# A PSUM bank for each direction in the block merges of a triangular inverse

## The chip, the cores and the metric

The kernel runs on one core of one Trainium2 chip. The metric is the device time of one execution in microseconds (us); of several runs the median counts.

## What is computed

One layer of a bidirectional hybrid encoder on x (1024 tokens, 1024 channels, float32): an input projection feeds eight heads of neighbourhood attention and four heads of gated DeltaNet in two directions; both are mapped by an output projection, and a mixture of 64 experts (two per token) follows. The change lies in the DeltaNet part. Per direction, head and chunk of 64 tokens the reference solves a unit lower triangular system and carries a state over the chunks:

```python
lower = jnp.where(strict, jnp.einsum('bhnid,bhnjd->bhnij', kb, k) * decay, 0.0)
a_mat = jnp.eye(c, dtype=f32) + lower
sol = lax.linalg.triangular_solve(a_mat, rhs, left_side=True, lower=True, unit_diagonal=True)
u, w = sol[..., :dv], sol[..., dv:]
def step(state, inp):
    v_new = u_c - jnp.einsum('bhck,bhkv->bhcv', w_c, state)
    o_c = (jnp.einsum('bhck,bhkv->bhcv', q_c * jnp.exp(g_c)[..., None], state)
           + jnp.einsum('bhij,bhjv->bhiv', qk_c, v_new))
    state = (state * jnp.exp(g_last)[..., None] + ...)
```

## The kernel before

The kernel is one long function, recorded in source order and then put in order by a scheduler: on each engine instructions may stand far from their source neighbours, and once that order is fixed each engine works through it strictly, so that an instruction which waits holds up all behind it. Which PSUM tiles share a bank, and what depends on what, enters into the scheduler's order. So an edit of a few lines can move instructions of other stages.

The kernel inverts the 64x64 triangular matrices itself. VectorE (DVE) inverts the two 32x32 diagonal blocks of 64 matrices (16 chunks by 4 heads) for each of the two directions by substitution (L457, L460). Then come the **merges**: the off-diagonal 32x32 block is minus the product of three 32x32 blocks. The 64 matrices go in four groups g of 16. Stage one of a group is 32 small matmuls, 16 of direction 0 (L483, operands in partitions 0 to 31, result in PSUM partitions 32 to 63) and 16 of direction 1 (L484, operands in 96 to 127, result in 64 to 95), in alternation. ScalarE (ACT, L485) and DVE (L486) copy the results to `wt`. Stage two is the same with L489 and L490, and ACT (L491) and DVE (L492) write the block to `TT`. A DMA on GpSimd's queue (POOL, L493) stores the group to `T_d` in DRAM. A stage's results of both directions share one PSUM bank `pw` or `px`, taken in turn from the pool `psB` of five.

The matmuls of the **natural projections** (L84, L85, L86 in `mm3`) fill TensorE (PE) meanwhile; their weights are loaded by SP (L74, `w_raw`) and split by ACT (L75) and DVE (L76). Their q and k blocks are normalised: ACT squares (L402), DVE reduces (L403, L404), POOL takes the power -0.5 (L51, the function `rsqrt`), DVE scales (L406), PE transposes (L417), and ACT and DVE take the result out of PSUM (L421, L422).

After the merges comes the **scan** over 16 chunks, a chain: PE multiplies the state (`pk`, L529), DVE makes `r` (L531, eight instructions), PE multiplies by the inverse (`pw`, L536), ACT and DVE copy the result (`wc`, L537 and L538), PE makes the state's update (`ps`, L545), DVE the new state (`sn`, L551). Outputs (L559, L556, L563) and the natural projections lie between. Attention, the output projection, the router and the experts come after.

Of the kernel before, what the change touches and what calls it, by code (L numbers as in the profile page):

```python
# [8 lines left out]
F32 = mybir.dt.float32  # L9
# [3 lines left out]
AF = mybir.ActivationFunctionType  # L13
OP = mybir.AluOpType
# [5 lines left out]
P = 128  # L20
# [16 lines left out]
def tile_layer(ctx, tc, a, out):  # L37
    nc = tc.nc
    pe, act, dve, pool, sp = nc.tensor, nc.scalar, nc.vector, nc.gpsimd, nc.sync
# [27 lines left out]
    psB = psP.enter_context(tc.tile_pool(name="psB", bufs=5, space=PSUM, side="right"))  # L67
# [32 lines left out]
    for t in range(NT):  # L100
# [11 lines left out]
        if t % 4 == 3:  # L112
            t0 = t - 3
            for k in range(NK):
                pt = psB.tile([P, 4, P], F32, name="pB")
                for j in range(4):
# [6 lines left out]
                                         op0=OP.mult, op1=OP.subtract)  # L123
# [316 lines left out]
    cb = cbp.tile([P, NH, 32], F32, name="cb")  # L440
# [23 lines left out]
    with tc.tile_pool(name="ty", bufs=1, side="right") as ty:  # L464
        TT = ty.tile([P, NH, CH], F32, name="TT")
        XdT = ty.tile([P, NH, 32], F32, name="XdT")
        wt = ty.tile([P, NH, 32], F32, name="wt")
        pool.memset(TT[32:64, :, 0:32], 0.0)
        pool.memset(TT[64:96, :, 32:64], 0.0)

        for m0, m1 in ((0, 16), (16, 64)):
            for d in range(2):
                for b in range(2):
                    p0 = d * 64 + b * 32
                    pool.dma_start(TT[p0:p0 + 32, m0:m1, b * 32:b * 32 + 32],
                                   X_d[d, d * 64 + m0:d * 64 + m1, b].rearrange("m p q -> p m q"))
                    sp.dma_start(XdT[p0:p0 + 32, m0:m1], X_d[1 - d, d * 64 + m0:d * 64 + m1, b].rearrange("m p q -> p m q"))
        for g in range(4):
            ms = range(g * 16, g * 16 + 16)
            gs = slice(g * 16, g * 16 + 16)  # L480
            pw = psB.tile([P, 16, 32], F32, name="pB")
            for m in ms:
                pe.matmul(pw[32:64, m % 16], cb[0:32, m], XdT[0:32, m], start=True, stop=True)  # L483
                pe.matmul(pw[64:96, m % 16], cb[96:128, m], XdT[96:128, m], start=True, stop=True)  # L484
            act.activation(wt[32:64, gs], pw[32:64], AF.Copy)  # L485
            dve.tensor_copy(wt[64:96, gs], pw[64:96])  # L486
            px = psB.tile([P, 16, 32], F32, name="pB")
            for m in ms:
                pe.matmul(px[0:32, m % 16], wt[32:64, m], TT[32:64, m, 32:64], start=True, stop=True)  # L489
                pe.matmul(px[96:128, m % 16], wt[64:96, m], TT[64:96, m, 0:32], start=True, stop=True)  # L490
            act.activation(TT[0:32, gs, 32:64], px[0:32], AF.Copy, scale=-1.0)  # L491
            dve.tensor_scalar(TT[96:128, gs, 0:32], px[96:128], -1.0, None, op0=OP.mult)  # L492
            pool.dma_start(T_d[:, g * 4:g * 4 + 4], TT[:, gs].rearrange("p (n h) c -> p n h c", h=DH))  # L493
    inv.close()
    psP.close()
# [12 lines left out]
    for n in range(NCH):  # L508
# [14 lines left out]
        else:  # L523
# [3 lines left out]
            for d in range(2):  # L527
                for h in range(DH):
                    pe.matmul(pk[d][:, h], qkT[:, h, step(d, n)], st[:, d, h], start=True, stop=True)  # L529
                for h in range(DH):  # L530
                    dve.scalar_tensor_tensor(r[hf[d], h], pk[d][hf[0], h], nE[hf[d], n, h:h + 1], vn[hf[d], h],  # L531
                                             op0=OP.mult, op1=OP.add)
        pw = psK.tile([P, DH, DD], F32, name="pw")
# [428 lines left out]
    wt = {}  # L962
# [279 lines left out]
```

## Time and profile before

| | before |
|---|---|
| median of 3 runs | 1382.51 us (1381.34 to 1383.73) |
| the profiled execution, its own time | 1388.08 us |
| its span | 1386.4 us |
| busy: PE, DVE, ACT, POOL | 1177.5, 643.5, 375.8, 381.9 us |
| PE's share of the span | 85% |
| mean granted clock of TensorE | 0.938 of full speed |

All rows further down are from the one profiled execution; it took 5.6 us more than the median of the others, so a difference worked out from its rows is added to the median. Busy times are sums over stages with different limits, so the stage of the change has to be looked at by itself. "Granted clock" is the share of TensorE's full clock (2.4 GHz) that the chip allowed in a stretch; 0.50 is its lower level, 1.2 GHz.

### The profile page before, as it was taken

What the parts mean: (1) busy time and instruction counts of PE and PEld (TensorE: products, weight loads), DVE (VectorE), ACT (ScalarE), POOL (GpSimd) and SP (SyncE); (2) the same over time, 40 slices, a digit from 0 to 9 for tenths busy, and PEclk for the clock granted to TensorE, in tenths of its full rate; (3) what the DMA queues carried; (4) which work ended last, traced back from release to release, by engine and by line L of the source; (5) the groups of instructions that cost most, each with busy time, mean ns of one, the idle gap of its engine ahead of it and who ended that gap; (6) DMA issues with size and microseconds to landing.
All of it is one profiled execution on the core that took longest, in us unless ns stands there. A gap on an engine that the chain in (4) does not pass through costs nothing. (4 is left out here: it accounts for less than half of the span.)

```text
span 1386.4 us, 21032 instructions
## 1 busy us (share of the span) xinstructions
PE 1177.5 (85%) x7427; PEld 821.7 (59%) x7428; DVE 643.5 (46%) x1615; ACT 375.8 (27%) x768; POOL 381.9 (28%) x433
## 2 busy tenths in 40 slices
PE   6977999979989896679989968887887788868885
PEld 6866889979889895467768853333332333323332
DVE  5556863763466633667867962122211212122211
ACT  6435432322244423665545310000000000000000
POOL 1147313013567463121210352111212112212111
PEclk9989999988999997899999969999998999989999
DMA  4251246346666497998692979999999999998991
GB/s 160 67 116 48 66 143 166 97 135 137 198 184 163 124 251 199 261 266 206 166 265 104 334 307 357 398 409 400 398 404 397 353 391 406 393 372 333 402 383 54
DMA packets 109954, 347.13 MB, mean 250 GB/s; under 512 B 43104, under 2 KB 49248, under 8 KB 93168
## 3 DMA queue, kind: packets, MB, share of 16 engines
q1 hardware_dynamic: 74480, 260.68, 52.2%
q0 software_dynamic: 27056, 68.79, 19.2%
q10 hardware_dynamic: 8272, 15.78, 3.2%
q8 instruction: 83, 1.36, 0.4%
q14 instruction: 63, 0.52, 0.1%
HBM read 305.26 MB, written 61.67 MB: 265 GB/s over the span
## 5 line engine op out<-in xcount | busy, mean ns | idle before, releaser
L1037 PE MATMUL pp<-wg,xT 128*64 128x512 f32 x1024 | 229.7, 598 | 17.7 <-DVE xT L1026 16.7
L1072 PE MATMUL po<-wd,hT 128*64 128x512 f32 x512 | 128.2, 632 | 44.2 <-DVEq L1151 31.7
L1037 PEld LDWEIGHTS pp<-wg,xT 128*64 128x64 f32 x1024 | 72.3, 137 | 153.3 <-issue 130.4
L84 PE MATMUL pA<-w_hi,h_hi 128*128 128x256 f32 x512 | 151.2, 295 | 0.0
L86 PE MATMUL pA<-w_hi,h_lo 128*128 128x256 f32 x512 | 149.2, 291 | 0.0
L85 PE MATMUL pA<-w_lo,h_hi 128*128 128x256 f32 x512 | 148.9, 291 | 0.0
L1053 POOL DMA_INDIRECT out<-yg,tS x32 | 50.8, 1586 | 287.0 <-DVE yg L1074 243.3
L1041 DVE SCALAR_TENSOR_TENSOR sg<-pp,tS,sg 128x256 f32<-128x256 f32 x32 | 15.5, 484 | 229.9 <-ACTq L1151 185.8
L1072 PEld LDWEIGHTS po<-wd,hT 128*64 128x64 f32 x512 | 42.8, 144 | 129.9 <-issue 67.8
L1074 DVE TENSOR_SCALAR yg<-po,tS 128x512 f32<-128x512 f32 x64 | 46.7, 749 | 125.2 <-DMA out<-yg,tS 62.9
L84 PEld LDWEIGHTS pA<-w_hi,h_hi 128*128 128x128 f32 x512 | 101.1, 197 | 0.4 <-issue 0.2
L85 PEld LDWEIGHTS pA<-w_lo,h_hi 128*128 128x128 f32 x512 | 100.9, 197 | 0.0
L86 PEld LDWEIGHTS pA<-w_hi,h_lo 128*128 128x128 f32 x512 | 100.6, 196 | 0.1
L1040 ACT ACTIVATE sg<-pp,tS 128x256 f32<-128x256 f32 x32 | 15.1, 473 | 267.5 <-PE pp L1037 267.5
L84 PE MATMUL pA<-h_hi,w_hi 128*128 128x512 f32 x192 | 76.7, 399 | 0.0
L85 PE MATMUL pA<-h_lo,w_hi 128*128 128x512 f32 x192 | 76.6, 399 | 0.0
L86 PE MATMUL pA<-h_hi,w_lo 128*128 128x512 f32 x192 | 76.0, 396 | 0.0
L76 DVE TENSOR_TENSOR w_lo<-w_raw,w_hi 128x512 fp32r<-128x512 f32 x56 | 39.1, 714 | 72.6 <-ACT w_hi L75 71.0
L250 DVE SCALAR_TENSOR_TENSOR acc<-raw,convw,acc 128x1024 f32<-128x1024 f32 x48 | 63.2, 1319 | 11.5 <-ACT acc L248 11.1
L1049 ACT ACTIVATE hT<-ph 128x256 f32<-128x256 f32 x32 | 12.3, 384 | 193.4 <-PE ph L1047 193.4
L84 PE MATMUL pA<-wo_hi,t_hi 128*128 128x512 f32 x128 | 55.0, 429 | 7.1 <-ACT t_hi L746 5.3
L661 PE MATMUL pv<-pT,vw 128*128 128x256 f32 x192 | 54.3, 419 | 3.3 <-ACT pT L652 2.4
(338 smaller groups left out, 2329.4 us busy)
## 6 DMA issues: line engine op xcount, KB each, us to landing
wg<-in_w_gu SPq DMA_DIRECT2D x62, 2048.0 KB
wd<-in_w_down SPq DMA_DIRECT2D x63, 1024.0 KB
bt<-in_bias SPq DMA_DIRECT2D x24, 384.0 KB
w_raw<-in_w_nat SPq DMA_DIRECT2D x32, 256.0 KB
w_raw<-in_w_dn SPq DMA_DIRECT2D x24, 256.0 KB
k<-kk_d POOLq DMA_DIRECT2D x16, 384.0 KB
SA_d<-cm POOLq DMA_DIRECT2D x8, 512.0 KB
kk_d<-ev POOLq DMA_DIRECT2D x8, 512.0 KB
```

The costliest lines, as they stand in the source:

```text
L76: dve.tensor_sub(lo[:, k:k + 2], raw, hi[:, k:k + 2].bitcast(F32))
L84: pe.matmul(dst, sh, mh, start=(i == 0), stop=False)
L85: pe.matmul(dst, sh, ml, start=False, stop=False)
L86: pe.matmul(dst, sl, mh, start=False, stop=(i == n - 1))
L250: dve.scalar_tensor_tensor(acc, raw[:, t:t + S], convw[:, m, t:t + 1], acc, op0=OP.mult, op1=OP.add)
L661: pe.matmul(pv, vw[:, w, half + g, pr * P:(pr + 1) * P], pT[:, g], start=(g == 0), stop=(g == 2))
L1037: pe.matmul(pp[d * CAP:(d + 1) * CAP], xT[:, k, d * CAP:(d + 1) * CAP], ws[d][0][:, :, k * 256:(k + 1) * 256], start=(k == 0), stop=(k == ...
L1040: act.activation(sg[:n], pp[:n, 0], AF.Silu, scale=mf[:n, 3:4])
L1041: dve.scalar_tensor_tensor(sg[:n], pp[:n, 1], mf[:n, 3:4], sg[:n], op0=OP.mult, op1=OP.mult)
L1053: ins = pool.indirect_dma_start(out=out, out_offset=bass.IndirectOffsetOnAxis(ap=idx, axis=0), in_=yg, in_offset=None, bounds_check=S - 1, ...
L1072: pe.matmul(po[d * CAP:(d + 1) * CAP], hT[:, k, d * CAP:(d + 1) * CAP], w[1][:, k * D + c * 512:k * D + (c + 1) * 512], start=(k == 0), st ...
L1074: dve.tensor_scalar(yg[:n, cs], po[:n], mf[:n, 2:3], None, op0=OP.mult)
```

## The change

Each direction gets a PSUM tile of its own. `pw` and `px` become lists of two tiles of `psB`; direction 0 writes the first, direction 1 the second. The partitions within the tiles, the operands and the arithmetic stay. A blank line makes every line behind it one higher (L483 is L484, L551 is L552).

```diff
-            pw = psB.tile([P, 16, 32], F32, name="pB")
+
+            pw = [psB.tile([P, 16, 32], F32, name="pB") for d in range(2)]
             for m in ms:
-                pe.matmul(pw[32:64, m % 16], cb[0:32, m], XdT[0:32, m], start=True, stop=True)
-                pe.matmul(pw[64:96, m % 16], cb[96:128, m], XdT[96:128, m], start=True, stop=True)
-            act.activation(wt[32:64, gs], pw[32:64], AF.Copy)
-            dve.tensor_copy(wt[64:96, gs], pw[64:96])
-            px = psB.tile([P, 16, 32], F32, name="pB")
+                pe.matmul(pw[0][32:64, m % 16], cb[0:32, m], XdT[0:32, m], start=True, stop=True)
+                pe.matmul(pw[1][64:96, m % 16], cb[96:128, m], XdT[96:128, m], start=True, stop=True)
+            act.activation(wt[32:64, gs], pw[0][32:64], AF.Copy)
+            dve.tensor_copy(wt[64:96, gs], pw[1][64:96])
+            px = [psB.tile([P, 16, 32], F32, name="pB") for d in range(2)]
             for m in ms:
-                pe.matmul(px[0:32, m % 16], wt[32:64, m], TT[32:64, m, 32:64], start=True, stop=True)
-                pe.matmul(px[96:128, m % 16], wt[64:96, m], TT[64:96, m, 0:32], start=True, stop=True)
-            act.activation(TT[0:32, gs, 32:64], px[0:32], AF.Copy, scale=-1.0)
-            dve.tensor_scalar(TT[96:128, gs, 0:32], px[96:128], -1.0, None, op0=OP.mult)
+                pe.matmul(px[0][0:32, m % 16], wt[32:64, m], TT[32:64, m, 32:64], start=True, stop=True)
+                pe.matmul(px[1][96:128, m % 16], wt[64:96, m], TT[64:96, m, 0:32], start=True, stop=True)
+            act.activation(TT[0:32, gs, 32:64], px[0][0:32], AF.Copy, scale=-1.0)
+            dve.tensor_scalar(TT[96:128, gs, 0:32], px[1][96:128], -1.0, None, op0=OP.mult)
```

The scheduler answers with another order. On PE, in group 0 of the merges, stage one stands so before (pB is any tile of `psB`; after the last row the alternation goes on until both directions have 16):

```order
L86 MATMUL pA<-w_hi,h_lo 128x256
L483 MATMUL pB<-XdT,cb 32x32
L84 MATMUL pA<-w_hi,h_hi 128x256
...
L86 MATMUL pA<-w_hi,h_lo 128x256
L484 MATMUL pB<-XdT,cb 32x32
L483 MATMUL pB<-XdT,cb 32x32
L484 MATMUL pB<-XdT,cb 32x32
L483 MATMUL pB<-XdT,cb 32x32
```

In the order before, one matmul of direction 0 stands alone, 39 projection matmuls follow, and then the directions alternate. The same place on PE now (old line numbers plus one), stages one and two:

```order
L86 MATMUL pA<-w_hi,h_lo 128x256
L484 MATMUL pB<-XdT,cb 32x32 x16
L84 MATMUL pA<-w_hi,h_hi 128x256
...
L485 MATMUL pB<-XdT,cb 32x32 x16
L490 MATMUL pB<-TT,wt 32x32 x16
L85 MATMUL pA<-w_lo,h_hi 128x256
L86 MATMUL pA<-w_hi,h_lo 128x256
L491 MATMUL pB<-TT,wt 32x32 x16
```

Here the 16 matmuls of a direction stand in a row, with nothing of the other direction between them. In group 1 it is the same (stage two: 14 and 14 in a row, then two pairs); in groups 2 and 3 stage one still alternates, and stage two begins with 5 and 5, and 6 and 6, in a row.

The second place is the scan, on DVE, chunk steps 3 to 4. Before (the numbers of `pk`, `ps` tell the steps apart):

```order
L531 SCALAR_TENSOR_TENSOR r<-pk_2534,nE,vn 64x128 x4
L404 TENSOR_SCALAR rsn<-rsn 128x8
L406 TENSOR_TENSOR qn<-pA,rsn 128x512
L538 COPY wc<-pw 128x256
L551 TENSOR_TENSOR sn<-ps_2560,sn 128x512
L551 TENSOR_TENSOR sn<-ps_2561,sn 128x512
```

Now at the same step:

```order
L532 SCALAR_TENSOR_TENSOR r<-pk_2542,nE,vn 64x128 x4
L403 TENSOR_REDUCE rsn<-qn 128x8
L539 COPY wc<-pw 128x256
L404 TENSOR_SCALAR rsn<-rsn 128x8
L406 TENSOR_TENSOR qn<-pA,rsn 128x512
L422 SCALAR_TENSOR_TENSOR ev_4599<-pA,qkg,ev_4599 128x512
L552 TENSOR_TENSOR sn<-ps_2568,sn 128x512
L552 TENSOR_TENSOR sn<-ps_2569,sn 128x512
```

The three instructions of the normalisation moved from between `r` and the copy `wc` to between the copy and the new state `sn`. This pattern stands in steps 1, 4, 7, 10 and 13 of the changed order. Before, the stretch between `wc` and `sn` held in five of the steps one or two instructions of L403, L404, L422 or L76, in step 0 all four, and never L406. PE's order is the same in both from the last projection blocks after the scan on, the other engines' from early in the attention on.

## Rows read from the trace of the kernel before

**Rows 1.** Stretches: us, busy (instructions) by engine; at the end granted clock, DMA share, GB/s.

```profile
337.00:350.50 13.50, 12.04 (x405) 11.23 (x403) 8.44 (x13) 6.00 (x10) 5.43 (x6) 0.75 0.51 162
360.60:486.70 126.10, 114.19 (x1010) 108.41 (x1011) 85.25 (x210) 53.42 (x156) 74.19 (x84) 0.96 0.60 158
486.70:545.00 58.30, 47.84 (x369) 46.68 (x368) 18.92 (x43) 9.37 (x16) 31.73 (x37) 0.90 0.95 221
```

**Rows 2.** Whom PE waited for, 300 to 545 us: total, times, longest.

```profile
PE pB L483 <- DMA XdT<-X_d: 9.8, 1, 9.8
PE pk L529 <- DVE sn L551: 5.4, 4, 3.2
PE ps L545 <- ACT wc L537: 3.2, 2, 2.2
PE ps L545 <- DVE wc L538: 2.4, 2, 1.5
PE pB L484 <- issue: 0.8, 1, 0.8
PE pB L489 <- ACT wt L485: 0.7, 1, 0.7
```

**Rows 3.** Timeline of PE in group 0: start, us, what; 32 records of L484 in all.

```profile
316.80 0.21 PE L484 MATMUL pB<-XdT,cb 32*32 32x32 f32 x1
316.81 0.21 PE L483 MATMUL pB<-XdT,cb 32*32 32x32 f32 x1
...
317.77 0.22 PE L484 MATMUL pB<-XdT,cb 32*32 32x32 f32 x2
...
318.98 0.28 PE L86 MATMUL pA<-w_hi,h_lo 128*128 128x256 f32 x1
319.19 0.24 PE L489 MATMUL pB<-TT,wt 32*32 32x32 f32 x2
...
319.59 0.28 PE L85 MATMUL pA<-w_lo,h_hi 128*128 128x256 f32 x1
```

**Rows 4.** Timeline of ACT and DVE, the copies of group 0.

```profile
318.03 0.59 ACT L485 ACTIVATE wt<-pB 32x512 f32<-32x512 f32 x1 [0.88 <-PE pB L484]
318.65 0.69 DVE L486 COPY wt<-pB 32x512 f32<-32x512 f32 x1 [9.07 <-ACT wt L485]
```

**Rows 5.** Stretches of 1 us in groups 1 to 3, columns as in rows 1.

```profile
341.00:342.00 1.00, 0.52 (x34) 0.40 (x25) 0.97 (x2) 0.59 (x1) 0.00 (x0) 1.00 0.51 74
342.00:343.00 1.00, 0.70 (x33) 0.70 (x34) 0.97 (x2) 0.00 (x0) 0.00 (x0) 0.50 0.96 307
348.00:349.00 1.00, 1.00 (x6) 1.00 (x7) 0.00 (x0) 0.00 (x0) 0.46 (x1) 0.59 1.03 387
```

**Rows 6.** Timeline of scan step 2, which has nothing inserted.

```profile
379.38 0.42 DVE L538 COPY wc<-pw 128x256 f32<-128x256 f32 x1 [1.19 <-ACT wc L537]
379.51 1.16 PE L545 MATMUL ps<-wc,kd 64*128 64x128 f32 x16
380.78 1.29 DVE L551 TENSOR_TENSOR sn<-ps,sn 128x512 f32<-128x512 f32 x2 [0.97 <-PE ps L545]
381.60 1.97 PE L529 MATMUL pk<-sn,qkT 128*128 128x128 f32 x16
```

**Rows 7.** The normalisation's links: POOL's L51 by its line (min/median/max ns), DVE's by the timeline.

```profile
L51 POOL TENSOR_TENSOR rsn<-rsn,mhalf x10: 1632/1670/1739, 333.0 to 494.9; 128x8 f32<-128x8 f32 x10
332.76 0.17 DVE L404 TENSOR_SCALAR rsn<-rsn 128x8 f32<-128x8 f32 x1
371.26 0.69 DVE L406 TENSOR_TENSOR qn<-pA,rsn 128x512 f32<-128x512 f32 x1 [1.85 <-POOL rsn L51]
346.67 0.75 DVE L422 SCALAR_TENSOR_TENSOR ev<-pA,qkg,ev 128x512 f32<-128x512 f32 x1
```

**Rows 8.** Timeline: the longest wait of the scan, on DVE and on PE.

```profile
413.52 0.69 DVE L76 TENSOR_TENSOR w_lo<-w_raw,w_hi 128x512 fp32r<-128x512 f32 x1 [2.53 <-ACT w_hi L75]
414.87 3.78 PE L529 MATMUL pk<-sn,qkT 128*128 128x128 f32 x16 [3.24 <-DVE sn L551]
```

## The prediction

> **What bounds the kernel now.** I read the stretches of the merges, the scan and what follows first [rows 1]. TensorE is busy 12.04 of 13.50 us in groups 1 to 3 of the merges, 114.19 of 126.10 us in the scan and 47.84 of 58.30 us behind it: with projection matmuls as filler PE is the bound, and what ends later is later by PE's own work, by the waits that filler doesn't cover, and by the granted clock. The list of PE's waits [rows 2] names the rest: 9.8 us for the first XdT load, which the change doesn't touch; only 0.7 us for the ACT copy of the merges and 0.8 us without a named cause; in the scan 5.4 us for the new state (L529 on L551) and 5.6 us for `wc`. Then the timeline of a merge, of a scan step without inserted work, and of the longest stall.
>
> Behind the scan PE has the same filler and the same order in both kernels, and the attention begins from PE's last projection blocks. So I let a shift at the scan's end pass whole to the end.
>
> **The eviction, which the diff is about.** With a shared bank DVE starts its copy (318.65) when ACT's has ended (318.03 + 0.59 = 318.62) [rows 4]; with banks apart both can run at once, 0.6 us earlier in each of eight stages. But PE waited for such copies only 0.7 us [rows 2], since filler covers them. So at most 0.7 us of these 4.8 is on the path.
>
> **The matmuls of the merges.** In the alternating order the two directions run side by side: 316.80 and 316.81 are the first of each, and the 32 records (two per instruction) of L484 are begun by 317.80, so one direction's 16 instructions take 1.0 us and the other's cost nothing more [rows 3]. The pitch, 31 ns, is that of one direction in its own corner of the array, and I take it for 16 in a row as well. Now 16 in a row are followed by 16 of the other direction: 2.0 us instead of 1.0. Four stages (both of groups 0 and 1) lose 1.0 us each, less 0.1 for the two pairs left in group 1; stage two of group 2 loses 5/16 and of group 3 6/16, 0.7 together: +4.6 us of PE time. Bounds: 0, if the second direction's instructions start while the first's run, and 4.6, since a direction's own weight loads are already in the pitch.
>
> The Trainium skill, "TensorE: Matmul & The Clock Gate", Part 3 (Packing small matmuls), says that matmuls start and end in strict program order; by that a block of 16 can't be overtaken by the next and the whole 4.6 us falls due. The same part says that a weight load overlaps running matmuls only where the row group differs. The trace disagrees: 16 full-array records of L529 with changing weights take 1.97 us [rows 6], 0.12 us each.
>
> Switching between small and full matmuls costs too: from 318.98 to 319.59 stand L86, one L489 and one L84 [rows 3], 0.61 us, where two projection matmuls 0.12 us apart take 0.24 and the two records 0.06: 0.31 for going there and back. The old order has eight such visits, the new one seven: -0.3 us.
>
> Waits: the 0.7 and 0.8 us go (the stages of group 1 are fed from results that are older or have 14 matmuls between); -1.5. In group 2 the copy (0.59 and some 0.3 of latencies) has one projection matmul and half a switch as cover: +0.5. Sum of the merges at full clock: 4.6 - 0.3 - 1.5 + 0.5 = **+3.3 us**.
>
> **The clock in the merges.** After small matmuls with two gaps (busy 0.52 of the microsecond from 341) the granted clock falls from 1.00 to 0.50 at 342.0 and comes back at about 348.6 [rows 5]: 6.6 us at half speed, 3.3 us lost. The new order has the same groups in one piece, with 2.5 us more of small matmuls and half of the gaps. If small matmuls keep the clock up, the fall vanishes: -3.3. If they don't, the extra work lies in the fall and costs double, and the clock returns later: up to +6. The nearest row is from 342 to 343, busy 0.70 with nearly nothing but small ones and still at 0.50, so I lean to a fall: **+2.0 us** (this holds 0.5 for group 0, where 16 small matmuls now stand at the half clock that follows the XdT wait).
>
> **The scan.** In step 2, `wc` ends on DVE at 379.80, the new state begins at 380.78, 0.98 later, its first half is done about 381.43, and PE takes it up at 381.60 without a wait [rows 6]: state and PE meet with next to no slack. In steps 1, 4, 7, 10 and 13 of the new order DVE has L404, L406 and L422 in that place, and L406 waits for POOL's L51, which waits for L404: 0.17 + 0.1 + 1.67 + 0.69 + 0.67 (0.75 less the overlap with its successor) = 3.3 us [rows 7] instead of 0.98, so the state is 2.3 us late. PE's order has two more projection matmuls ahead of L529 there, and a little more before: 0.3 us. 2.0 us a step, 10.0 in all. Against that, the old order has L404, L51 and L406 mostly between `r` and `wc` and pays 11.0 us for state and `wc` [rows 2]; 3.2 and 2.2 of it (the two longest) are other waits, of which the first is DVE's L76 for a late weight load [rows 8]. So 5.6 us go and 10.0 come: **+4.4**. Bounds 0 (the power is ready earlier than I think) and +6 (nothing of the old goes).
>
> The weight loads: L76 stands before the state of step 6 as before, so the 3.24 us stay; at the end of the scan it stands behind the outputs, which may save 1.0 of the 2.2; in step 5 a new one may cost 0.5. **-0.5**. The long stalls took the clock down as well: L529 took 3.78 us behind the one of 3.24 [rows 8] against 1.97. Five more stalls of 2 us may do that again, one more fall of 3 us at half speed in excess of a lesser one gone: **+1.0**, between -2 and +6.
>
> **Sum.** 3.3 + 2.0 + 4.4 - 0.5 + 1.0 = +10.2 us. Against the profiled execution's own 1388.08 us that is 1398.3; against the median of 1382.51, which counts, **1392.7 us**.
>
> **Rivals.**
> First, the clock holds in the merges, since small matmuls are work too and the gaps are fewer: -3.3 instead of +2.0, 1387.4 us. For it: the gaps of 1.5 us ahead of the old fall; against it: the row from 342.
> Second, the scan swallows the new order: POOL's power is done under other work and the state isn't late, so 4.4 and 1.0 fall away, and with the clock of the first rival little is left: 1382.5 to 1385. For it: PE's order has some filler more in these steps; against: L406 waited 1.85 us for L51 in the old order too [rows 7].
> Third, faster: the shared bank holds the old merges back. Then banks apart make each stage shorter than its 1.0 us, the copies run side by side, and the fall of the clock goes: half of the eight stages' 8.0 us, 1.5 of waits and 3.3 of clock, -8.8; less 4.4 that the scan gives back, 1378 us. It decides only if stages in a row come out under 0.5 us a direction. Against it: pairs start 10 ns apart in one bank [rows 3].
> The Trainium skill, "TensorEngine Tiling (Array Packing)", Restrictions and Gotchas, states this rival's mechanism: different row tiles can't access the same PSUM bank at the same time. By that rule the change would win the time above; these rows show two row tiles side by side in one bank, in different partitions, so here the rule doesn't bear.
>
> **Chances.** Forecast (both costs, +5 to +17) 0.60; clock holds 0.18 (+3 to +7); scan swallows it 0.13; faster 0.09. The range that leaves out no more than 2 in 10: **1383.5 to 1400**; the forecast's own 1388 to 1399. A measurement of this kernel tells about 0.2% (2.8 us) from no change. Faster by more: 0.08; within: 0.13; slower: 0.79.
>
> **What would show it.** In the changed profile: the 16 matmuls of L484 and those of L485 one block behind the other, 1.0 us each at full clock; ACT's and DVE's copies starting together; the granted clock at 0.50 for 7 us or more from about 345; in steps 1, 4, 7, 10, 13 DVE idle some 1.8 us before L406, and PE 2 us before L530, released by the state. Wrong I am if the blocks overlap, if the clock stays up, or if the waits for the state stay near 5 us; and if the scan ends 10 us later but the attention doesn't begin so, the shift was slack.

## The result and the profile after

The changed kernel took 1393.45 us (median of 6 runs, 1392.47 to 1400.54) beside 1383.3 us before: a ratio of 1.0064, with a 95% interval of 1.0039 to 1.009, or 8.9 us more (the two medians lie 10.2 us apart; the ratio with its interval is what counts). Timed again later, beside other runs of before, the ratio was 1.0044 (1.0022 to 1.0065). It is slower, by 6 to 9 us. The profiled execution took 1393.21 us, its span is 1391.5 us.

Stretches of the changed kernel from the landing of XdT to the scan, the scan up to its last state, and what follows (columns as in [rows 1]):

```profile
309.70:366.50 56.80, 56.65 (x795) 55.11 (x796) 15.08 (x24) 12.02 (x21) 18.67 (x21) 0.82 0.63 158
366.50:485.80 119.30, 105.12 (x940) 98.95 (x940) 80.58 (x197) 48.16 (x142) 72.57 (x81) 0.97 0.61 159
485.80:545.00 59.20, 52.71 (x433) 51.46 (x431) 23.04 (x55) 14.10 (x27) 31.33 (x39) 1.00 0.94 222
```

The same stretches of merges and scan in the kernel before, PE alone (length, PE busy and instructions, granted clock, DMA share, GB/s):

```profile
309.60:362.30 52.70, 50.72 (x805) 0.89 0.70 170
362.30:479.30 117.00, 105.14 (x944) 0.97 0.62 164
```

Between XdT and the first `wc` PE now has nearly no idle time (0.15 us; 1.98 before), ten records fewer, and still takes 4.1 us more: the mean clock fell from 0.89 to 0.82. Whom PE waited for from 300 to 545 us, as in [rows 2]:

```profile
PE pk L530 <- DVE sn L552: 12.0, 6, 3.4
PE pB L484 <- DMA XdT<-X_d: 10.5, 1, 10.5
PE pA L417 <- DVE qn L406: 2.7, 3, 1.1
PE ps L546 <- ACT wc L538: 1.1, 3, 0.5
PE ps L546 <- DVE wc L539: 0.9, 2, 0.5
PE pB L490 <- ACT wt L486: 0.2, 1, 0.2
```

State and `wc` together cost 14.0 us of waits; they cost 11.0 in [rows 2]. The wait of L417 (the transposes) for `qn` isn't new: [rows 2] leave that line out, though in the same view of before its sum is the largest:

```profile
PE pA L417 <- DVE qn L406: 10.1, 3, 5.9
```

Its 5.9 us lie behind the attention's first matmul in both kernels, in the changed one at 547, outside the window. Ahead of the attention, behind the scan, it is 4.2 us before and 2.7 now. Of the merges' own waits, 0.8 and 0.7 us in [rows 2], 0.2 us is left.

**The blocks.** Timeline of PE, groups 0 and 1, the answer to [rows 3]:

```profile
309.67 1.88 PE L484 MATMUL pB<-XdT,cb 32*32 32x32 f32 x32 [10.46 <-DMA XdT<-X_d]
...
325.15 1.19 PE L484 MATMUL pB<-XdT,cb 32*32 32x32 f32 x32
326.27 0.38 PE L84 MATMUL pA<-w_hi,h_hi 128*128 128x256 f32 x1
```

The 32 records of one direction are one piece: 1.12 us from 325.15 to the next instruction at full clock, 1.81 us at half clock (309.67 to 311.48). In [rows 3] 62 of both directions' 64 records lay between 316.80 and 317.93, in the time of one such block. Blocks overlap only at their edges: the first three records of L490 begin at 319.41 to 319.50, among the last three of L485.

**The copies.** Timeline of ACT and DVE, group 2, the answer to [rows 4]:

```profile
344.53 0.59 ACT L486 ACTIVATE wt<-pB 32x512 f32<-32x512 f32 x1 [0.41 <-PE pB L485]
344.57 0.69 DVE L487 COPY wt<-pB 32x512 f32<-32x512 f32 x1 [0.29 <-PE pB L485]
```

They start 0.04 us apart, where DVE waited for ACT's end before. So the banks do what the change says; PE hardly waited there.

**The clock.** Stretches of 1 us, columns as in [rows 5]:

```profile
341.00:342.00 1.00, 1.00 (x40) 1.00 (x38) 0.40 (x1) 0.00 (x0) 0.00 (x0) 1.00 0.00 0
342.00:343.00 1.00, 1.00 (x32) 0.90 (x29) 0.97 (x2) 0.00 (x0) 0.00 (x0) 1.00 0.05 16
343.00:344.00 1.00, 1.00 (x68) 1.00 (x66) 0.44 (x2) 0.47 (x1) 0.00 (x0) 1.00 0.00 0
344.00:345.00 1.00, 1.00 (x31) 0.66 (x23) 0.71 (x2) 0.59 (x2) 0.17 (x1) 0.64 0.87 172
354.00:355.00 1.00, 1.00 (x7) 1.00 (x6) 0.78 (x2) 0.00 (x0) 0.37 (x1) 0.50 0.33 70
357.00:358.00 1.00, 1.00 (x7) 1.00 (x6) 0.00 (x0) 0.00 (x0) 0.00 (x0) 0.53 0.97 379
358.00:359.00 1.00, 1.00 (x10) 1.00 (x10) 0.00 (x0) 0.00 (x0) 0.00 (x0) 1.00 0.66 173
```

The fall comes at 344, behind three microseconds in which PE was busy throughout, mostly with small matmuls, and lasts to 358: 13.7 us at half speed. In [rows 5] it was 6.8 (from 342.0; the 0.59 of the microsecond from 348 puts its end at 348.8, where the prediction read 348.6).

**The scan.** Timeline of step 4, the counterpart of [rows 6] and [rows 7]:

```profile
398.23 0.42 DVE L539 COPY wc<-pw 128x256 f32<-128x256 f32 x1
398.57 0.16 DVE L404 TENSOR_SCALAR rsn<-rsn 128x8 f32<-128x8 f32 x1
398.82 1.67 POOL L51 TENSOR_TENSOR rsn<-rsn,mhalf 128x8 f32<-128x8 f32 x1 [2.26 <-DVE rsn L404]
400.52 0.69 DVE L406 TENSOR_TENSOR qn<-pA,rsn 128x512 f32<-128x512 f32 x1 [1.79 <-POOL rsn L51]
401.13 0.74 DVE L422 SCALAR_TENSOR_TENSOR ev<-pA,qkg,ev 128x512 f32<-128x512 f32 x1
401.79 1.28 DVE L552 TENSOR_TENSOR sn<-ps,sn 128x512 f32<-128x512 f32 x2
402.52 2.05 PE L530 MATMUL pk<-sn,qkT 128*128 128x128 f32 x16 [1.70 <-DVE sn L552]
```

The chain over POOL stands there as the order had it: DVE idle 1.79 us ahead of L406, PE 1.70 us ahead of the state. Steps 1, 7, 10 and 13 show 1.87, 1.68, 1.69 and 1.66 us; the sixth wait (3.41) is the late weight load, as in [rows 8].

### The profile page after: what moved, and what is told of

The parts are those of the page before. It is cut to its first block, busy times and chain, and to the rows that moved or that the text cites. A ratio compares the mean times of both kernels' runs of the same rounds, so it can differ in the third digit from the quotient of the medians.

```text
span 1391.5 us, 21020 instructions
## 1 busy us (share of the span) xinstructions
PE 1184.2 (85%) x7427; PEld 830.0 (60%) x7428; DVE 645.9 (46%) x1615; ACT 375.5 (27%) x768; POOL 382.2 (27%) x433
## 3 DMA queue, kind: packets, MB, share of 16 engines
q1 hardware_dynamic: 74480, 260.68, 52.1%
## 5 line engine op out<-in xcount | busy, mean ns | idle before, releaser
L1038 PEld LDWEIGHTS pp<-wg,xT 128*64 128x64 f32 x1024 | 75.5, 138 | 153.9 <-issue 124.8
L1073 PE MATMUL po<-wd,hT 128*64 128x512 f32 x512 | 124.6, 615 | 42.6 <-DVEq L1152 27.9
L1054 POOL DMA_INDIRECT out<-yg,tS x32 | 50.8, 1586 | 284.6 <-DVE yg L1075 236.4
L76 DVE TENSOR_TENSOR w_lo<-w_raw,w_hi 128x512 fp32r<-128x512 f32 x56 | 40.0, 728 | 74.8 <-ACT w_hi L75 73.0
```

Source lines behind the costliest of these rows:

```text
L76: dve.tensor_sub(lo[:, k:k + 2], raw, hi[:, k:k + 2].bitcast(F32))
L1038: pe.matmul(pp[d * CAP:(d + 1) * CAP], xT[:, k, d * CAP:(d + 1) * CAP], ws[d][0][:, :, k * 256:(k + 1) * 256], start=(k == 0), stop=(k == ...
L1054: ins = pool.indirect_dma_start(out=out, out_offset=bass.IndirectOffsetOnAxis(ap=idx, axis=0), in_=yg, in_offset=None, bounds_check=S - 1, ...
L1073: pe.matmul(po[d * CAP:(d + 1) * CAP], hT[:, k, d * CAP:(d + 1) * CAP], w[1][:, k * D + c * 512:k * D + (c + 1) * 512], start=(k == 0), st ...
```

## The experiments

All ratios are to runs of the kernel before on the same chip. The table has three stretches of each profile, in us, with the time lost to a lower granted clock in brackets (the sum of 1 minus the clock over stretches of 1 us): from PE's start on XdT to ACT's first `wc`, on to the last state that PE takes up, and on to the attention's first matmul (L635 before).

| kernel | ratio (95%) | XdT to `wc` | scan | to attention | sum |
|---|---|---|---|---|---|
| before | 1 | 52.3 (6.0) | 117.4 (3.8) | 49.1 (2.3) | 218.8 |
| e0, before again | one execution | 50.7 (5.1) | 115.5 (1.7) | 47.7 (0) | 213.9 |
| changed | 1.0064 (1.0039, 1.009) | 56.4 (10.5) | 119.8 (3.4) | 48.4 (0) | 224.5 |
| g3, changed again | 1.0044 (1.0022, 1.0065) | 57.3 (11.2) | 120.1 (5.1) | 48.3 (0) | 225.8 |
| e1 own banks, alternating | 1.0012 (0.9994, 1.003) | 55.0 (10.2) | 115.9 (3.4) | 48.7 (0.6) | 219.6 |
| e2 shared bank, blocks | 1.0078 (1.0056, 1.0099) | 62.9 (13.8) | 116.4 (1.7) | 48.4 (0) | 227.6 |
| e3 changed, state first | 1.0019 (1.0001, 1.0037) | 56.2 (10.3) | 112.9 (1.7) | 48.1 (1.1) | 217.2 |
| f2 shared, alternating, scan tied | 0.9925 (0.9904, 0.9946) | 50.8 (5.2) | 107.8 (0) | 44.8 (0) | 203.3 |
| f3 own, blocks, scan tied | 0.9983 (0.9967, 0.9999) | 56.2 (10.3) | 109.1 (0) | 46.2 (0) | 211.5 |
| f1 own, alternating, scan tied | 0.9924 (0.9895, 0.9954) | 50.4 (3.0) | 110.8 (1.7) | 44.7 (0) | 206.0 |
| f4 as f2, merges spread | 0.995 (0.9928, 0.9972) | 61.1 (4.4) | 105.6 (0) | 42.3 (0) | 209.0 |
| g1 before, chain in the scan | 0.9997 (0.998, 1.0015) | 52.1 (5.6) | 118.9 (0) | 44.4 (0) | 215.4 |
| g2 as g1, weights tied | 0.996 (0.9944, 0.9976) | 51.4 (5.4) | 119.5 (0) | 41.8 (1.7) | 212.6 |
| g4 as g1, with L422 | 1.0002 (0.9982, 1.0022) | 51.3 (5.3) | 115.8 (0) | 46.7 (0) | 213.8 |

### Is it the bank or the order?

Run e2 keeps the shared bank and writes the two directions one behind the other; the blocks, and a scan in nearly the changed kernel's order, follow.

```diff
             for m in ms:
                 pe.matmul(pw[32:64, m % 16], cb[0:32, m], XdT[0:32, m], start=True, stop=True)
+            for m in ms:
                 pe.matmul(pw[64:96, m % 16], cb[96:128, m], XdT[96:128, m], start=True, stop=True)
... (stage two, `px`, likewise)
```

> One bank for both directions as before, but the loop over m written twice, one direction behind the other; merges in blocks of 16 and a scan in nearly the changed kernel's order follow. Theory 'order': 1393 us as changed, between 1390 and 1397, with the chain ahead of the state in five steps; ACT's and DVE's copies one behind the other. Rival 'banks': 1383 us as before. If sharing held merges back, as the rival of a faster change had it, it would be slower than the changed kernel by 4 us or more.

It took 1397.16 us, 1.0078: as slow as the changed kernel with no second bank in it (0.0014 more, 1.9 us, with some 4.6 us either way, so that a price of sharing of a few us is left to f1, below). Its copies stand one behind the other (ACT and DVE in group 0, timeline):

```profile
318.13 0.59 ACT L486 ACTIVATE wt<-pB 32x512 f32<-32x512 f32 x1 [0.64 <-PE pB L485]
...
318.75 0.69 DVE L487 COPY wt<-pB 32x512 f32<-32x512 f32 x1 [10.66 <-DMA TT<-X_d]
```

Run e1 is the other half: own banks, with the matmuls tied into alternation by edges that only set the order.

```diff
-                pe.matmul(pw[0][32:64, m % 16], cb[0:32, m], XdT[0:32, m], start=True, stop=True)
-                pe.matmul(pw[1][64:96, m % 16], cb[96:128, m], XdT[96:128, m], start=True, stop=True)
+                x = pe.matmul(pw[0][32:64, m % 16], cb[0:32, m], XdT[0:32, m], start=True, stop=True)
+                if m % 16:
+                    order_after(x, last, "the directions alternate")
+                y = pe.matmul(pw[1][64:96, m % 16], cb[96:128, m], XdT[96:128, m], start=True, stop=True)
+                order_after(y, x, "the directions alternate")
+                last = y
... (stage two, `px`, likewise)
```

> Own banks kept, the matmuls of the two directions tied into the alternating order of before; the scan gets a third order (normalisation's L406 behind the state or 0.7 us ahead of it, no chain over POOL there). Theory 'order' (banks cost nothing in themselves; blocks in a row and the chain ahead of the state cost): no block in the merges, one clock fall of 3.4 us as before, waits for the state under 8 us: 1380 us, between 1376 and 1386. Rival 'banks' (the second bank itself costs): 1393 us as changed. Rival 'merges only' (the scan's order costs nothing): 1384 to 1387.

It took 1388.02 us, 1.0012, not told from before, though outside the expected 1376 to 1386: without the blocks and with a third order of the scan, most of the loss is gone. But the forecast of one short fall was wrong: the clock was down from 340 to 358 here (8.5 us lost). The order of its stages differs from before's, so the banks' own share is read better from f1, below.

### The state ahead of the normalisation

Run e3 is the changed kernel with L406 and L422 of the five blocks behind the second `sn` of their step; the scheduler then puts L406 between the state and `r`, and L422 behind `r`.

```diff
+    behind = {3: 1, 4: 4, 5: 7, 6: 10, 7: 13}
...
-        dve.tensor_tensor(qn, pv, rs[:, 2, :, None].to_broadcast([P, 8, AD]), op=OP.mult)
+        x = dve.tensor_tensor(qn, pv, rs[:, 2, :, None].to_broadcast([P, 8, AD]), op=OP.mult)
+        behind_state(x, len(norms))
+        norms.append(x)
```

> The changed kernel with own banks and blocks in the merges; in the scan the products and the second halves of the turn (L406, L422) of five blocks are tied behind the new state of their step. Theory 'order': the merges stay 5 us longer than before, the waits for the state fall from 12.0 us to under 5: 1384 us, between 1380 and 1388. Rival 'merges only': 1393 us. Rival 'scan is PE-bound' (waits go elsewhere): 1390 to 1393, with the gain turned into other waits.

It took 1386.95 us, 1.0019. The waits for the state fell from 12.0 to 6.0 us, not under 5 (3.9 of which is one late weight load), the scan from 119.8 to 112.9 us, the merges stayed as they were. So the chain does cost, in this scan; what before's own scan costs beside it is another question, below.

### The merges by themselves

Runs f2, f3 and f1 have one and the same set of ties in the scan: those of e3, and the weight halves' L76 behind the state of their step as well. f2 is the kernel before, f3 the changed one, f1 own banks in alternation.

```diff
+    weights = {48: 0, 49: 0, 50: 5, 51: 6, 52: 12, 53: 12, 54: 13, 55: 13}
...
-            dve.tensor_sub(lo[:, k:k + 2], raw, hi[:, k:k + 2].bitcast(F32))
+            x = dve.tensor_sub(lo[:, k:k + 2], raw, hi[:, k:k + 2].bitcast(F32))
+            if len(lows) in weights:
+                tc.add_manual_dep(x.ins, states[weights[len(lows)]].ins.name, mybir.DependencyInfo(mybir.DependencyClass.NoSync, mybir.DependencyReason.DATA),
+                                  reason="the state is more urgent")
+            lows.append(x)
```

> The kernel before with its shared bank and alternating merges; in the scan L406, L422 and the weight halves' L76 are tied behind the state of their step. It is the base for the next three, which have the same ties. Theory 'order': the waits for the state and for wc fall from 11.0 us to under 5: 1379 to 1381 us, ratio 0.996 (0.993 to 0.999). Rival 'scan is PE-bound': 1384 to 1386, ratio 1.000.

> The changed kernel (own banks, blocks in the merges) with the scan tied as in the base. What it takes more than the base is the merges' price by itself. Theory 'order': 4 to 6 us more than the base, of which the longer fall of the granted clock is more than half. Rival 'scan only' (the merges cost nothing): within 1.5 us of the base.

> Own banks with the matmuls tied into alternation, and the scan tied as in the base. Theory 'order' in its first form (the blocks make the fall of the clock longer): within 1.5 us of the base. Rival 'density' (the fall is longer wherever the stages of groups 1 to 3 come with few full matmuls between them, alternating or not, as it was 8.5 us of loss in the first run with own banks and alternation): 3 to 5 us more than the base, with the clock low until 355 us or later.

Measured: 1374.11, 1382.59 and 1375.88 us. f3 less f2 is the merges' price: 0.9983 - 0.9925 = 0.0058, 8.0 us, and with the two intervals taken as independent about 3.7 us either way. f1 and f2 are the same (0.9924 and 0.9925, some 5 us either way): two banks in themselves cost and bring nothing that can be measured. Their stretches from XdT to `wc`, first f2, PE alone:

```profile
307.90:358.70 50.80, 49.27 (x801) 0.90 0.67 171
```

then f3, PE alone:

```profile
310.40:367.00 56.60, 56.45 (x794) 0.82 0.65 161
```

The expected 4 to 6 us were too few, though in the interval; by the profiles the stretch is 5.4 us longer with 11 projection matmuls fewer in it (their order has 260 ahead of the scan's first matmul, not 271), and the sum to the attention 8.2 us (211.5 and 203.3). Of the 5.4 us, 5.1 are lost to the clock (10.3 and 5.2). Not all of the 8.2 us is the merges': the 11 matmuls done later are 1.3 us, but DVE's order in the two scans is not the same in spite of the ties, and PE waits 1.4 us more in f3 between the merges and the attention (4.6 us in the scan and 3.7 behind it; 3.8 and 3.3 in f2). The merges themselves come to 5.4 + 1.3 = 6.7 us.

f2 gained more than expected, since hardly anything in the scan waits any longer. Whom PE waited for in f2's scan:

```profile
PE ps L562 <- ACT wc L554: 1.7, 4, 0.5
PE pw L553 <- DVE r L548: 0.8, 1, 0.8
PE ps L562 <- DVE wc L555: 0.5, 1, 0.5
PE ps L562 <- POOL kd L537: 0.5, 1, 0.5
```

The state isn't in the list (0.2 us for it follow at its end), and the granted clock stayed at 1.00 throughout the scan. f2 and f1 beat both kernels by 10 us and more.

How long the clock is down in the merges: the six profiles with before's merges (before, e0, f2, g1, g2, g4) each have one fall that costs 3.4 us, begun between 338 and 343; the four with the changed ones (changed, e3, f3, g3) one of 6.8 us, begun between 344 and 346 (g3 another of 1.7 us, from 322); e2's longer blocks 10.2 us. On PE the six have one and the same order from XdT to the scan, and so have the four. The six stretches take 50.7 to 52.3 us (51.4 on average, 5.4 of them lost to the clock), the four 56.2 to 57.3 (56.5 and 10.6). With 1.3 us for the 11 matmuls, the blocks cost 6.4 us by these ten profiles, 5.2 of it by the clock. The order of e1 and f1, one and the same on PE in the merges, has two outcomes. First e1, PE in two stretches of 10 us:

```profile
340.00:350.00 10.00, 9.76 (x164) 0.51 0.72 241
350.00:360.00 10.00, 10.00 (x111) 0.64 0.46 141
```

then f1, which has the same merges:

```profile
340.00:350.00 10.00, 9.00 (x338) 1.00 0.49 158
350.00:360.00 10.00, 9.67 (x109) 1.00 0.79 254
```

The same instructions once lose 8.5 us and once nothing, so the order of the small matmuls alone doesn't settle the fall.

Run f4 was to spread them: on f2, three stages are tied behind later projection matmuls.

```diff
+        ties = {(1, 1): 1448, (2, 0): 1472, (3, 0): 1502}
...
+                if m % 16 == 0 and (g, 0) in ties:
+                    behind_full.setdefault(ties[g, 0], []).append(x)
```

> The base with the first matmuls of groups 1 (stage two), 2 and 3 tied behind later projection matmuls, so that 24 and more full matmuls stand between the groups of the merges. If the small matmuls close together take the clock down, the fall after 340 us goes or gets shorter: 3.4 us less than the base or a part of it. If any stage takes it down, the fall comes as in the base, or comes twice: 0 to 3 us more.

1377.13 us, 0.995: 3.4 us more than f2, less than the 4.2 us that the intervals leave open. The fall is shorter (342 to 346, 1.7 us lost), but the ties brought a wait of 3.5 us of L417 for `qn` into the merges, ahead of that very fall, so the run is inconclusive about what takes the clock down.

### The scan by itself

Run g1 is the kernel before with only the scan tied: L404 behind `wc`, and `sn` behind L406 and L422, in steps 1, 4, 7, 10 and 13. g2 adds the ties of the weight halves, so that it compares with f2. g4 is g1 with L422 tied behind `wc` too and so into the same place, which gives DVE's order in the scan as the changed kernel has it, but for L76, L403 and the turns within the chain.

```diff
+        if len(norms) in ahead:
+            order_after(x, wcs[ahead[len(norms)]])
+            for z in firsts[ahead[len(norms)]]:
+                order_after(z, y)
```

> The kernel before with its bank and merges; only the scan is tied so that L404 and L406, with L51 on POOL between them, stand between wc and the state in steps 1, 4, 7, 10 and 13, as in the changed kernel. It is the scan's term by itself. As predicted (+4.4 for the chain net of what before pays for wc): 4 to 5 us slower than before, ratio 1.003. Rival 'before's own scan order costs as much': ratio 1.000 to 1.001, since tying the state first took 0.75% off before's merges and 0.8% off the changed ones.

> As the last, with the weight halves' L76 tied behind the state as in the base (f2_shared_alternate, 0.9925). Against that base only the place of the normalisation differs: five times L404, L51, L406 ahead of the state (and once more in step 14). At 2.0 us a step: 10 to 12 us more than the base, ratio 1.000 to 1.001. If PE's filler covers the chain: under 4 us more, 0.993 to 0.995.

> As g1_chain_in_before, with the second half of the turn (L422, 0.67 us) tied into the same place too, as in the changed kernel: L404, L422, L406 between wc and the state in steps 1, 4, 7, 10 and 13. The first of these runs came to 0.9997. If the scan as the changed kernel has it costs the predicted 4.4 us: ratio 1.002 to 1.004, steps of 9.3 us and 12 to 14 us of waits for the state. If the scan's term is nothing even so, the whole change lies in the merges: 0.999 to 1.001.

Measured: 1385.42, 1381.75 and 1386.51 us; 0.9997, 0.996 and 1.0002. The predicted 4.4 us aren't there: the changed kernel's scan, as nearly as g4 has it, costs 0.3 us on before's merges, between -2.5 and 3.1. g3, on the same chip, is the changed kernel whole: 1.0044 less 1.0002 is 5.8 us, some 4.0 either way, a second price of the merges beside f3 less f2. Whom PE waited for in g4's scan:

```profile
PE pk L544 <- DVE sn L566: 10.4, 7, 2.9
PE ps L560 <- ACT wc L552: 1.4, 4, 0.5
PE ps L560 <- POOL kd L535: 0.7, 1, 0.7
PE ps L560 <- DVE wc L553: 0.5, 1, 0.5
```

The chain is paid (10.4 us for the state), but before's order pays nearly as much in its own way: 5.4 for the state and 5.6 for `wc` [rows 2]. And behind the scan L417 waits 2.2 us for `qn` in g4, 4.2 in before. g2 against f2 prices it without that set-off, for five chains and a sixth in step 14: 0.996 - 0.9925 = 0.0035, 4.9 us by the ratios, about 3.7 either way, 7.6 by the medians (on two chips, whose runs of before lie 1.0 us apart), and 9.3 by the two profiles' sums to the attention. The 10 to 12 expected were too much by the ratios, but the chain does cost, and not the under 4 us of PE covering it.

### Both kernels again

> The kernel before, unchanged, for a second profile: the profiled execution of before took 1388.08 us and its median is 5 us less. If the extra 5 us are one fall of the granted clock (from 526 to 534 us), this profile shows 1382 to 1384 us and no such fall; if they lie in the expert phase, the time up to 850 us is the same in both profiles.

> The changed kernel again, for a second profile and a narrower ratio beside the same runs of before: 1.0064 as the first time (1.004 to 1.009); in the profile the same fall of the clock from about 344 to 358 us and waits for the state of 11 to 13 us.

e0 took 1386.14 us with falls of the clock at other places: 1.7 us lost in the scan and 1.7 from 525, where the first profile lost 3.8 in the scan and 4.7 between its end and 535. It reaches the attention 4.5 us earlier (523.9 and 528.4), and ends only 1.9 us earlier. So neither case that was expected is what it shows; profiles of one kernel differ by such falls, one or two of 1.7 to 3.4 us each, and a difference of a few us between two single profiles is no finding. g3 repeated the changed kernel's profile: the fall from 346 to 360, and

```profile
PE pk L530 <- DVE sn L552: 11.3, 6, 2.7
```

## Why the prediction was right, point by point

The forecast was 1392.7 us, 10.2 above the median; 1393.45 and 8.9 us came. Direction, size and the main cause (the order, not the bank) hold. The split between merges and scan does not: 5.3 of the 10.2 us were put on the merges and 4.9 on the scan, and the runs give 8.0 (f3 less f2, 3.7 either way; 6.4 by ten profiles) and 0.3 (g4, -2.5 to 3.1). That the sum came so near is in part luck: a scan term that is too large makes up for merges that are too small.

- **The eviction.** Right: both copies start together, and it is worth nothing, as f1 beside f2 shows.
- **De-interleaving, +4.6, with visits -0.3.** The mechanism is right: a direction's 16 are a block of 1.12 us, and blocks overlap by no more than their edges. The size comes out smaller: PE's busy time less the time lost to the clock is 56.65 - 10.5 = 46.2 us now and 50.72 - 6.0 = 44.7 before; with 11 projection matmuls of 0.12 us moved out, 1.3 us, the small ones cost 2.8 us more, not 4.3. Part of that gap is the bookkeeping: a block at half clock takes 1.81 us, not twice 1.12, so the clock's loss is counted a little too high.
- **Waits of the merges, -1.0 in sum.** Right in kind: 1.98 us of idle PE became 0.15, -1.8.
- **The clock in the merges, +2.0.** Mis-sized: 10.5 - 6.0 = 4.5 us in the profiled pair, 3.4 of it the longer fall, the same in six profiles against four, and the rest group 0's, where the clock comes back at 317, not at 315. The lean to a fall was right, the reason for it only in part: the fall comes behind a stretch without gaps. The sum of these, 2.8 - 1.8 + 4.5 = 5.5 us, is the forecast's 5.3 with its parts traded; it lies below the 6.4 of ten profiles and the timed 8.0, within the interval of the latter.
- **The scan's chain, +4.4.** The step that failed: the term is too large. The chain stands as forecast (five steps, L51 1.67 us, DVE idle 1.79), with PE 1.7 us late in a step, not 2.0: 8.6 us instead of 10.0. "5.6 us go" holds in the waits: of the 14.0 us for state and `wc` 5.4 aren't the chain's, as 5.4 of the old 11.0 were to stay. So the waits rise by 3.0 us, not 4.4, and in time no more than that is left: g4 gives 0.3 us (-2.5 to 3.1). In a scan that waits for hardly anything the chain does cost some 5 to 9 us (g2); in before's it replaces waits nearly as long. A part may also come back behind the scan, where the prediction let a shift pass whole: L417 waits 4.2 and 4.4 us for `qn` in the two profiles of before (the first and e0), 2.7 and 2.9 in those of the changed kernel. No run isolates this part. The bound for "nothing of the old goes" would be +10 by the prediction's own numbers, not +6.
- **Weight loads -0.5, clock in the scan +1.0.** The wait for the weights stayed (3.41 us). Lost to the clock in the scan: 3.8 and 1.7 us before, 3.4 and 5.1 after. With two profiles of each, +1.5 us on average is no finding.
- **A shift passes whole to the end.** Borne out on average: from XdT to the attention the changed kernel takes 225.2 us (two profiles), before 216.4: 8.8 us; the ends of these four lie 7.0 us apart, and the timings say 8.9 and 6.1. But it isn't one shift passed on: the changed order has 14 more projection matmuls between scan and attention (315 and 301), and waits less for `qn` there.
- **The rivals.** The clock didn't hold in the merges. That the scan swallows its new order turned out true of its time, but not by the rival's mechanism: POOL's power isn't done under other work (DVE idle 1.79 us), and the state is late. The faster case fell with e2 and f1: the shared bank held nothing back, and the rule that different row tiles can't access one bank at a time (the Trainium skill, "TensorEngine Tiling (Array Packing)", Restrictions and Gotchas) doesn't bear here: the two directions' records start 10 ns apart in one bank [rows 3], and f1, with the banks apart, takes f2's time.

What stays open: why the fall in the merges is longer with blocks. It was so in every profile with these blocks, but e1 and f1 show one order with and without a fall, and f4 brought a wait of its own. Open, too, is how much of the chain's wait comes back behind the scan.

## What to carry to other kernels

An edit that looks like a pure relief (a bank for each writer) goes through the scheduler: look at the order that it leaves before counting what the relief brings, and tie the good order where it matters. Small matmuls that use different corners of the array cost half here if their streams alternate. In a chain like this scan, let work that isn't the chain's (here products that wait for POOL, and weight halves that wait for a load) stand behind the next link on its engine: that took 0.75% off before, and with f1, which has the same ties, it is the best of the versions here.

## What was not expected of the hardware

TensorE's clock fell to its lower level (0.50, 1.2 GHz) after three microseconds in which it had been busy 1.00 of each, with small matmuls (341 to 344); the same small matmuls in the same order left it at 1.00 in one execution and took it down for 17 us in another (f1, e1). At the lower level 32 small records took 1.81 us and at the full 1.12, a factor of 1.6, not 2. And two engines that read two PSUM banks at once take no longer for it: ACT's copy 0.59 us and DVE's 0.69 us, the same as one behind the other.
